# Splitting half of an output-projection weight during attention and keeping the parts in DRAM

## The chip, the cores and the metric

The kernel runs on one core of one Trainium2 chip. The metric is the device time of one execution in microseconds (us): before the change the median of three runs is 1147.73 us (1147.73 to 1148.61).

## The reference

One decoder block for 1024 tokens of 1024 features, in float32:

```python
h = rms_norm(x, g_attn_pre) * (1 + sc_a) + sh_a        # sc_a, sh_a, gt_a, ... from cond @ w_ada
proj = h @ w_in                                        # queries, keys, values of 16 heads
oa = banded_attention(qa, ka, va, 127, sink)           # mixer A: window, sink, 8 heads
ob = dilated_mixture_attention(qb, kb, vb)             # mixer B: 8 heads
mixed = concatenate([rms_norm(oa, g_mix_a), rms_norm(ob, g_mix_b)])
x = x + gt_a * rms_norm(mixed @ w_out, g_attn_post)
h = rms_norm(x, g_mlp_pre) * (1 + sc_m) + sh_m
x = x + gt_m * rms_norm(square(relu(h @ w_up)) @ w_down, g_mlp_post)
```

`w_out` is 1024 x 1024. The kernel folds the gains `g_mix_a`, `g_mix_b` into its rows.

## The kernel before

**Two parts for every number.** TensorE multiplies in a reduced format, so each operand is kept as a high part (the value rounded) and a low part (the rest), and every product takes three matmuls: high by high, low by high, high by low. Making the parts of a tile is called a split here: ScalarE (ACT) writes the high part, and VectorE (DVE), or GpSimd (POOL) where it is free, subtracts it from the value for the low part.

**Stages.** First the modulated, normalised `h` is made, transposed, and split into the tile `hw`, which has eight places of two parts of 128 x 1024. Then 18 projection tiles per half of the tokens (six units `u`, each of three 128-column tiles `c`, for two halves `x` of 512 tokens) are accumulated over eight chunks `k` of 128 features (`proj_mm`, lines 859 to 869, output tile `pj`). The attention of what is projected already runs beside it: scores (`s_ps`, L1127 for mixer B, L1182 for A), the running maximum on DVE (L1146, L1197), the exponential on ACT (L1153, L1202), the division on POOL (L1158, L1214), transposes on TensorE (PE; L1232 and L1235, L1239), the split of the transposed weights (`ph`: ACT L1246, DVE L1250), the product with the values (L1262 to L1267, L1274), and the sum of two halves into `ot` (ACT L1294 or L1309, DVE L1298 or L1314), stored to DRAM (`o_dram`, L1301, L1319). Projected tiles are rotated on DVE (L762 to L765), split (ACT L768, DVE or POOL L771), and sent through DMAs (L808) to the query and key tiles. POOL also works off 24 pieces of the modulation matrix beside attention (`ada_piece`: load L999, L1010 to L1015). After the last projection tile comes the output projection: per 128 tokens `o_sb` is loaded back from DRAM (L1423), split into `oh` and `ol` (ACT L1436, DVE L1439) and multiplied with the parts of `w_out` (`y_ps`, L1478 to L1480). Then follows the MLP, more than half of the time, which the change leaves as it is.

**What the split of `w_out` does before.** `hw` holds `h` until the projection is done, and the parts of `w_out` afterwards, chunk `k` in place `k`. In the old layout place `b` holds the 128 tokens of block `b` for all eight feature chunks, so a half of the tokens frees its four places together, at the last chunk of the last projection tile of that half (line 931, resource `r_wo`). `load_wo` (L1339) then takes, for each of the eight chunks: a load of 0.5 MB into a staging place (`wo_st`, L1348), the high part on ACT (L1353), and the low part on DVE (L1356) or on POOL in two instructions (L1361, L1362), whichever its planner finds earlier.

**The staging ring.** Five places of 128 x 1024 (`stage`, L444) serve, one after the other, the rotated tiles `hl`, the pieces `wa_st`, the rows of the rotation tables, `gate_st`, and `wo_st`. The planner counts free places (`r_stg`); which physical place a new tile gets is decided by the allocator of the pool, and the first instruction that writes the tile then waits for whoever used that place last.

**What sets the order.** One Python planner (`Sched`) writes each engine's instructions from modelled durations: it takes the step that can start first. The order is fixed when the program is built; on the chip each engine works its list in order, and an instruction that waits holds up all that stand behind it on its engine. All DMAs of this stage are issued by one queue, SyncE's (SP), in its order.

Of the kernel before, what the change touches and what calls it, by code (L numbers as in the profile page):

```python
# [10 lines left out]
F32 = mybir.dt.float32  # L11
F32R = mybir.dt.float32r
# [3 lines left out]
ALU = mybir.AluOpType  # L16
# [3 lines left out]
P = 128  # L20
D = 1024
S = 1024
KC = D // P
# [151 lines left out]
class Sched:  # L175
# [144 lines left out]
def t_sb(n):  # L320
    return 0.098 + 0.00083 * n
# [6 lines left out]
def t_dv(n):  # L328
    return 0.066 + 0.00104 * n
# [19 lines left out]
def hybrid_block(ctx: ExitStack, tc: tile.TileContext, x, positions, w_ada, b_ada, g_attn_post, w_in, w_out,  # L349
                 g_mlp_post, w_up, w_down, consts, out):  # L350
    nc = tc.nc
    ctx.enter_context(tc.manual_schedule())
    V, A, G, T = nc.vector, nc.scalar, nc.gpsimd, nc.tensor
    x, out = x[0], out[0]
    w_ada, w_out, w_up, w_down = w_ada[0], w_out[0], w_up[0], w_down[0]
    sc = Sched()
    op, pe_op = sc.op, sc.pe_op

    def pool(name, bufs=1, side="left", space=None, stack=ctx):
        kw = dict(name=name, bufs=bufs, reuse_waits="tile")  # L360
# [8 lines left out]
    dram = ctx.enter_context(tc.tile_pool(name="dram", bufs=1, space=DRAM))  # L369
# [5 lines left out]
    def ring_r(name):  # L375

        return ph2.right.tile([P, 1024], F32, name=name, tag="right")
# [7 lines left out]
    r_stg, r_w, r_wst, r_hl = Res(5), Res(WR), Res(WS), Res(0)  # L385
    r_u, r_raw, r_h2, r_wo = Res(0), Res(0), Res(0), Res(0)
# [8 lines left out]
    cols = head[:, CW_COL - 8:CW_COL + 56]  # L395
# [26 lines left out]
    hw = pool("hw", 1).tile([P, KC, 2, 1024], F32R, name="hw")  # L422
# [16 lines left out]
    st = Tok()  # L439
# [28 lines left out]
    xnT = p0.tile([P, KC, S], F32, name="xnT")  # L468
# [56 lines left out]
    w_raw, w_rawe, w_hl, w_e = {}, {}, {}, {}  # L525
# [45 lines left out]
    e = op("ACT", 0.1, lambda: A.activation(cond[:], c_raw, AF.Exp, scale=-1.0), [e_c], prio=0)  # L571
# [32 lines left out]
    e = op("DVE", 4.2, f_turns, [e_pos, e_c], prio=1)  # L604

    def f_sin():
# [5 lines left out]
                prio=1)  # L612
# [26 lines left out]
    def mod_group(g):  # L639
# [37 lines left out]
    def mod_chunk(k, eg, half):  # L677
        t0, t1 = (0, TB) if half is None else (4 * half, 4 * half + 4)
        n = (t1 - t0) * P
        ks = slice(k * P, (k + 1) * P)  # L680
# [11 lines left out]
        e = op("DVE", t_dv(n), lambda: V.tensor_tensor(hw[:, t0:t1, 1, ks], h, hh.bitcast(F32), ALU.subtract), [e],  # L692
               prio=0)
        for x in (0, 1) if half is None else (half,):
            e_hh[k, x], e_hl[k, x] = eh, e
# [6 lines left out]
    def tables(groups, place, r_place, r_bank, bank, deps):  # L702
# [30 lines left out]
       prio=8)  # L733

    qs, ks, vs, e_q, e_k, n_in = {}, {}, {}, {}, {}, {}
# [117 lines left out]
    def dense(dur, emit, deps, **kw):  # L853
        return pe_op("dense", dur, emit, deps, **kw)

    def w_at(u, c, k):
        return divmod(3 * k + c, 4) if u == 0 else (2 * c + k // 4, k % 4)

    def proj_mm(ps, u, c, k, x, part):
        i, n = w_at(u, c, k)  # L860
        t, w = slice(k * P, (k + 1) * P), w_hl[u, i]
        n = slice(n * P, n * P + P)
        h = [hw[:, 4 * x:4 * x + 4, i, t] for i in range(2)]
        ps = ps[:].rearrange("p (b t) -> p b t", t=P)
        if part != 1:
            T.matmul(ps, w[:, 0, n], h[0], start=(k == 0), stop=False)  # L866
            T.matmul(ps, w[:, 1, n], h[0], start=False, stop=False)  # L867
        if part != 0:
            T.matmul(ps, w[:, 0, n], h[1], start=False, stop=(k == KC - 1))  # L869
# [74 lines left out]
    todo_dense = [(u, x, c) for u in range(1, 6) for x in range(2) for c in range(3)]  # L944

    def feed_proj():
        if len(sc.pe.get("dense", [])) <= 4 and todo_dense:
            u, x, c = todo_dense.pop(0)
            if (x, c) == (1, 0):
                next_unit_w(u)  # L950
            if (u, x, c) == (2, 0, 0):
                for e_ in e_tab:
                    e_.clear()
                tables([(0, 1, 4)], lambda i: stage("rows")[:].rearrange("p (b r) -> p b r", b=TB), r_stg, r_x,
                       lambda: px.tile([P, 4, P], F32, name="ptab", tag="x"), [[e_rot[1, 0]], [e_rot[1, 1]]])
            proj_tile(u, x, c)
        return not todo_dense
# [29 lines left out]
    NADA = 24  # L987
    ada = Tok()
# [347 lines left out]
    NSTG2 = 4  # L1336
    ph2 = Tok()

    def load_wo():  # L1339

        if len(todo_dense) > 2 or ada.i < NADA:
            return False
        ph2.e_wo, ph2.raw = {}, {}
        eh = None
        for k in range(KC):
            def f_l(k=k):
                ph2.raw[k] = stage("wo_st")
                nc.sync.dma_start(ph2.raw[k][:], w_out[k * P:(k + 1) * P])  # L1348
            e = load(f_l, 524288, takes=[(r_stg, 1), (r_wo, 1)], prio=-8)
            g = cols[:, 56 + k:57 + k]  # L1350

            def f_h(k=k, g=g):
                A.mul(hw[:, k, 0], ph2.raw[k][:], g)  # L1353

            def f_lo(k=k, g=g):
                V.scalar_tensor_tensor(hw[:, k, 1], ph2.raw[k][:], g, hw[:, k, 0].bitcast(F32), ALU.mult,  # L1356
                                       ALU.subtract)
            eh = op("ACT", t_sb(D) + AP_COST, f_h, [e] + ([eh] if eh else []), prio=4)

            def f_lo2(k=k, g=g):  # L1360
                G.tensor_scalar(ph2.raw[k][:], ph2.raw[k][:], g, 1.0, ALU.mult, ALU.mult)  # L1361
                G.tensor_tensor(hw[:, k, 1], ph2.raw[k][:], hw[:, k, 0].bitcast(F32), ALU.subtract)  # L1362
            ph2.e_wo[k] = op(("DVE", "POOL"), (t_dv(D) + AP_DV, t_pts(D) + t_ptt(D)), (f_lo, f_lo2), [eh],
                             gives=[(r_stg, 1)], prio=4)
        return True

    def open_out():
# [13 lines left out]
        return True  # L1381

    sc.launch += [load_wo, open_out]
    h2, e_h2 = {}, {}

# [694 lines left out]
```

## Time and profile before

| | |
|---|---|
| median of three runs | 1147.73 us (1147.73 to 1148.61) |
| the profiled execution | 1148.87 us |
| its span, first to last instruction | 1147.1 us (1.8 us lie around it) |
| mean granted TensorE clock | 0.992 |
| DVE, ACT, POOL busy | 71%, 55%, 23% of the span |
| PE busy | 97% |
| last projection matmul / first `y_ps` | 377 us / 398.38 us after the start |

A profile page gives busy times by engine and groups of equal instructions. A row of the timeline has start and duration in us, the engine, the line of the kernel, output and inputs by the program's names, the number of instructions, and in brackets how long the engine was idle just before and what ended that. Matmuls overlap: one of 512 columns takes 0.39 us, and the next starts 0.23 us after it. A row of the windows view has a stretch of time, its length, then for PE, PEld, DVE, ACT and POOL the busy time in it and the number of instructions, then the granted TensorE clock (1.00 is full speed), the busy share of the DMA engines and GB/s.

### The profile page before, as it was taken

The numbers are of one execution on the slowest core, as the hardware profiler recorded it, in microseconds if no ns is written. First come the engines' busy times: TensorE is split into PE (matmuls) and PEld (weight loads), VectorE is DVE, ScalarE is ACT, GpSimd is POOL, SyncE is SP. The second block draws the span as 40 slices with busy tenths as digits, with TensorE's granted clock in tenths as the row PEclk, the third lists the DMA queues.
The fourth block names the chain that finished last, engine by engine and source line by source line (L and its number), as shares of the span: only waits on it lengthen the run. The fifth ranks groups of instructions, "written<-read, shape, count | busy, mean of one in ns | idle before, by whom it ended". The sixth has DMA issues, their size and how long they took to land.

```text
span 1147.1 us, 15609 instructions
## 1 busy us (share of the span) xinstructions
PE 1115.2 (97%) x5417; PEld 924.1 (81%) x5417; DVE 818.7 (71%) x1380; ACT 635.9 (55%) x1101; POOL 265.7 (23%) x349
## 2 busy tenths in 40 slices
PE   8999999999999899998999999999999999999996
PEld 7788878888888687887788888888888888888885
DVE  7878666666667765668979664599644896537998
ACT  8868865464556756675675424563234733246542
POOL 2458867565743521111000000000000000000002
PEclk9999999999999899998999999999999999999999
DMA  9556454343423305552981168812469112584103
GB/s 347 192 204 164 163 158 164 136 155 127 146 71 132 124 26 186 203 207 104 352 306 39 41 224 285 303 37 74 147 230 332 70 56 76 201 307 168 37 19 147
DMA packets 90910, 185.29 MB, mean 162 GB/s; under 512 B 8400, under 2 KB 31056, under 8 KB 90832
## 3 DMA queue, kind: packets, MB, share of 16 engines
q1 hardware_dynamic: 90832, 184.30, 46.3%
q8 instruction: 43, 0.70, 0.2%
q14 instruction: 35, 0.29, 0.1%
HBM read 137.08 MB, written 28.31 MB: 144 GB/s over the span
## 4 chain that ended last, share of the span: by engine, by line
PE 76%; DVE 8%; issue 4%; ACT 4%; POOL 4%; DMA 3%; SPq 1%; DVEq 0%; POOLq 0%; ACTq 0%
PE mlp_ps L1903 16%; PE mlp_ps L1904 16%; PE mlp_ps L1902 16%; PE pj L866 3%; PE pj L869 3%; PE pj L867 3%; PE s_ps L1127 3%; PE o_ps L1262 2%; PE pt_ps L1232 1%; PE y_ps L1478 1%; PE y_ps L1480 1%; PE y_ps L1479 1%; PE pt_ps L1235 1%; DVE hw L1673 1%; PE o_ps L1267 1%
## 5 line engine op out<-in xcount | busy, mean ns | idle before, releaser
L1902 PE MATMUL mlp_ps<-hw 128*128 128x512 f32 x896 | 350.7, 391 | 0.4 <-ACT hw L1664 0.4
L1903 PE MATMUL mlp_ps<-hw 128*128 128x512 f32 x896 | 349.5, 390 | 1.1 <-DVE hw L1670 1.1
L1904 PE MATMUL mlp_ps<-hw 128*128 128x512 f32 x896 | 349.4, 390 | 0.0
L1903 PEld LDWEIGHTS mlp_ps<-hw 128*128 128x128 f32 x896 | 168.7, 188 | 36.9 <-DVE hw L1670 1.4
L1902 PEld LDWEIGHTS mlp_ps<-hw 128*128 128x128 f32 x896 | 168.8, 188 | 36.4 <-ACT hw L1664 0.8
L1904 PEld LDWEIGHTS mlp_ps<-hw 128*128 128x128 f32 x896 | 168.6, 188 | 35.0
L1673 DVE TENSOR_TENSOR hw<-w,hw 128x1024 fp32r<-128x1024 f32 x96 | 114.7, 1221 | 95.1 <-ACT hw L1666 93.0
L1666 ACT CAST hw<-w 128x1024 fp32r<-128x1024 f32 x96 | 97.5, 1047 | 129.8 <-PE mlp_ps L1904 93.1
L2002 POOL TENSOR_TENSOR st<-st,nhalf 128x1 f32<-128x1 f32 x8 | 7.8, 977 | 604.1 <-DVE st L2000 604.1
L866 PE MATMUL pj<-hw,w_hl 128*128 128x512 f32 x240 | 102.5, 427 | 0.0
L869 PE MATMUL pj<-hw,w_hl 128*128 128x512 f32 x240 | 94.6, 394 | 0.0
L867 PE MATMUL pj<-hw,w_hl 128*128 128x512 f32 x240 | 94.5, 394 | 0.0
L1250 DVE TENSOR_TENSOR ph<-pt_ps,ph 128x512 fp32r<-128x512 f32 (+1 forms) x110 | 69.5, 648 | 34.6 <-ACT ph L1246 34.3
L1666 ACT CAST hw<-u 128x1024 fp32r<-128x1024 f32 x48 | 48.7, 1051 | 64.6 <-PE mlp_ps L1904 64.6
L1246 ACT CAST ph<-pt_ps 128x512 fp32r<-128x512 f32 (+1 forms) x110 | 58.9, 555 | 32.9 <-PE pt_ps L1235 27.5
L1153 ACT ACTIVATE p_sb<-p_sb,mn 128x128 f32<-128x128 f32 (+3 forms) x64 | 49.8, 778 | 38.3 <-DVE mn L1146 36.8
L1673 DVE TENSOR_TENSOR hw<-u,hw 128x1024 fp32r<-128x1024 f32 x48 | 57.1, 1220 | 18.2 <-ACT hw L1666 18.2
L1960 DVE TENSOR_TENSOR yacc<-yacc,mlp_ps 128x512 f32<-128x512 f32 x96 | 62.2, 683 | 3.3 <-PE mlp_ps L1904 3.3
L1158 POOL TENSOR_SCALAR p_sb<-p_sb,den 128x128 f32<-128x128 f32 (+3 forms) x64 | 48.4, 762 | 53.1 <-DVE den L1156 51.9
L1015 POOL TENSOR_TENSOR ada_acc<-ada_acc,wa_st 128x512 f32<-128x512 f32 x42 | 55.3, 1318 | 3.5
L869 PEld LDWEIGHTS pj<-hw,w_hl 128*128 128x128 f32 x240 | 45.1, 188 | 10.5
L1478 PE MATMUL y_ps<-hw,oh 128*128 128x512 f32 x128 | 51.7, 404 | 0.0
(206 smaller groups left out, 2010.4 us busy)
## 6 DMA issues: line engine op xcount, KB each, us to landing
hw<-s_dram SPq DMA_DIRECT2D x84, 512.0 KB, 4.4
wa_st<-in_w_ada SPq DMA_DIRECT2D x32, 512.0 KB, 4.4
w<-in_w_up SPq DMA_DIRECT2D x32, 512.0 KB, 4.8
w<-in_w_down SPq DMA_DIRECT2D x32, 512.0 KB, 7.5
s_dram<-hw SPq DMA_DIRECT2D x28, 512.0 KB, 4.3
qt<-hl SPq DMA_DIRECT2D x40, 256.0 KB, 2.8
w_st<-in_w_in SPq DMA_DIRECT2D x36, 256.0 KB, 3.1
x_sb<-in_x SPq DMA_DIRECT2D x16, 512.0 KB, 6.1
```

The lines of the kernel that those rows point to most:

```text
L866: T.matmul(ps, w[:, 0, n], h[0], start=(k == 0), stop=False)
L867: T.matmul(ps, w[:, 1, n], h[0], start=False, stop=False)
L869: T.matmul(ps, w[:, 0, n], h[1], start=False, stop=(k == KC - 1))
L1246: A.copy(b["ph"][:, 0, :w], b["pt"][:, :w])
L1250: V.tensor_tensor(b["ph"][:, 1, :w], b["pt"][:, :w], b["ph"][:, 0, :w].bitcast(F32), ALU.subtract)
L1478: T.matmul(ps[:], b["oh"][:, k], wh[:, c0:c0 + 512], start=(k == 4 * m), stop=False)
L1666: A.copy(out[j][0], flat(src[j]))
L1673: V.tensor_tensor(out[j][1], flat(src[j]), out[j][0].bitcast(F32), ALU.subtract)
L1902: T.matmul(ps[m][:], sh, mh, start=starts and k == 0, stop=False, **kw)
L1903: T.matmul(ps[m][:], sh, ml_, start=False, stop=False, **kw)
L1904: T.matmul(ps[m][:], sl, mh, start=False, stop=k == 3, **kw)
L1960: e = op("DVE", t_dv(512), lambda: V.tensor_tensor(y(), y(), ps[m][:], ALU.add), [e, ml.e_y[tb, n]], gives=gives, prio=1)
```

## The change

Three things are changed.

1. `h` lies in `hw` by feature chunks: place `4x + k//2`, and there columns 512 (`k%2`) to 512 (`k%2`) + 511, hold chunk `k` of the 512 tokens of half `x`. Every second `k` of the last projection tile of a half frees one place.
2. Chunks 4 to 7 of `w_out` are split during the attention stage, one after the other, as soon as the projection has passed 2.2, 3.0, 3.8 and 4.6 units (`st.d` counts them). `split_wo` takes two staging places for a chunk: the raw values (`wo_st`), into which DVE later writes the low part, and `wo_hi`, into which ACT writes the high part. Both are stored to DRAM (`wo_dram`, two DMAs of 0.5 MB).
3. `load_wo` splits chunks 0 to 3 as before, with the low part on DVE only. Chunks 4 to 7 are loaded from DRAM by two DMAs of 0.5 MB each, as their places in `hw` come free.

```diff
 def mod_chunk(k, eg, half):
-        h, hh = xnT[:, k, t0 * P:t1 * P].rearrange("p (b t) -> p b t", t=P), hw[:, t0:t1, 0, ks]
+        h = xnT[:, k, t0 * P:t1 * P].rearrange("p (x t) -> p x t", t=512)
+        hh, hl = (hw[:, t0 // 4 * 4 + k // 2:t1 - 3 + k // 2:4, i, k % 2 * 512:k % 2 * 512 + 512] for i in range(2))
...
 def proj_mm(ps, u, c, k, x, part):
-        h = [hw[:, 4 * x:4 * x + 4, i, t] for i in range(2)]
-        ps = ps[:].rearrange("p (b t) -> p b t", t=P)
+        h = [hw[:, 4 * x + k // 2, i, k % 2 * 512:k % 2 * 512 + 512] for i in range(2)]
...
-            if u == 5 and c == 2 and k == KC - 1:
-                gives.append((r_wo, 4))
+            if u == 5 and c == 2 and k % 2:
+                gives.append((r_wo, 1))
...
+    def split_wo(k):
+        raw, hi = [], []
+        g = cols[:, 56 + k:57 + k]
+        def f_l():
+            raw.append(stage("wo_st"))
+            nc.sync.dma_start(raw[0][:], w_out[k * P:(k + 1) * P])
+        e = load(f_l, 524288, takes=[(r_stg, 1)], prio=21)
+        def f_h():
+            hi.append(stage("wo_hi"))
+            A.mul(hi[0][:].bitcast(F32R), raw[0][:], g)
+        eh = op("ACT", t_sb(D) + AP_COST, f_h, [e], takes=[(r_stg, 1)], prio=9)
+        def f_lo():
+            V.scalar_tensor_tensor(raw[0][:].bitcast(F32R), raw[0][:], g, hi[0][:], ALU.mult, ALU.subtract)
+        el = op("DVE", t_dv(D) + AP_DV, f_lo, [eh], prio=9)
+        e_wod[k] = [load(lambda t=t, i=i: nc.sync.dma_start(wo_dram[k - 4][i][:], t[0][:]), 524288, [e_],
+                         gives=[(r_stg, 1)], prio=22) for i, (t, e_) in enumerate(((hi, eh), (raw, el)))]
+    def feed_wo():
+        k = 4 + len(e_wod)
+        if st.d > WO_AT[k - 4]:
+            split_wo(k)
+        return len(e_wod) == 4
+    WO_AT = (2.2, 3.0, 3.8, 4.6)
...
-        for k in range(KC):
+        for k in range(4):
...
-            ph2.e_wo[k] = op(("DVE", "POOL"), (t_dv(D) + AP_DV, t_pts(D) + t_ptt(D)), (f_lo, f_lo2), [eh],
-                             gives=[(r_stg, 1)], prio=4)
+            ph2.e_wo[k] = op("DVE", t_dv(D) + AP_DV, f_lo, [eh], gives=[(r_stg, 1)], prio=4)
+        for k in range(4, KC):
+            def f_d(k=k):
+                for i in range(2):
+                    nc.sync.dma_start(hw[:, k, i].bitcast(F32), wo_dram[k - 4][i][:])
+            ph2.e_wo[k] = load(f_d, 1048576, e_wod[k], takes=[(r_wo, 1)], prio=-8, n=2)
```

The planner writes other orders from this. Lines behind 1338 have other numbers in the changed kernel: the split ahead is L1348 (load), L1353 (ACT), L1357 (DVE) and L1359 (stores) there, the load from DRAM L1395, `o_sb` L1455 and `oh` L1468; lines between 927 and 1335 are one lower than before (L1246 is L1245).

The first place is ACT about 144 us after the start, at the end of the rotation tables (`tab`), where the first tile `hl` of unit 2 is split. Before:

```order
L723 ACTIVATE tab_147<-ptab,head 128x512
L768 COPY hl<-hl 128x512
L1309 COPY otmp<-o_ps 64x512
L1246 COPY ph<-pt_ps 128x512 x2
L1202 ACTIVATE p_sb,den_1870<-p_sb,mn_1869 128x257 x4
L779 ACTIVATE hl<-pj,head 128x512
```

And in the change:

```order
L723 ACTIVATE tab_147<-ptab,head 128x512
L1353 ACTIVATE wo_hi<-wo_st,head 128x1024
L768 COPY hl<-hl 128x512
L1308 COPY otmp<-o_ps 64x512
L1245 COPY ph<-pt_ps 128x512 x2
L1201 ACTIVATE p_sb,den_1880<-p_sb,mn_1879 128x257 x4
```

The first split ahead stands in front of the split of `hl`, the copy `otmp` and the two `ph`.

The second place is SP at the same time. Before, behind the load of a modulation piece came the key tile, `o_dram` and `gate_st`:

```order
L999 DMA wa_st<-in_w_ada 128x2x512
L808 DMA kt<-hl 32x2x512
L1319 DMA o_dram_110<-ot 64x2x128 x2
L1039 DMA gate_st<-in_b_ada 128x512
L1040 DMA gate_st<-in_g_attn_post 128x512
L808 DMA kt<-hl 32x2x512
```

In the change the load of `wo_st` and the store of its high part stand between:

```order
L998 DMA wa_st<-in_w_ada 128x2x512
L1348 DMA wo_st<-in_w_out 128x1024
L1359 DMA wo_dram_0_174<-wo_hi 128x1024
L808 DMA kt<-hl 32x2x512
L1318 DMA o_dram_110<-ot 64x2x128 x2
L1038 DMA gate_st<-in_b_ada 128x512
L1039 DMA gate_st<-in_g_attn_post 128x512
L1359 DMA wo_dram_1_175<-wo_st 128x1024
```

Here `wo_st` is also taken from the staging ring ahead of the tile `hl` that L762 writes, where before `hl` was the next to be taken.

The third place is ACT from the last value tile (`v_hl`, 384 us) to the first `oh`. Before, with four splits of `w_out`:

```order
L844 COPY v_hl<-pv 128x8x64
L1353 ACTIVATE hw<-wo_st,head 128x1024
L1246 COPY ph<-pt_ps 128x512
L1353 ACTIVATE hw<-wo_st,head 128x1024
L1294 COPY otmp<-o_ps 64x256
L1246 COPY ph<-pt_ps 128x384
L1353 ACTIVATE hw<-wo_st,head 128x1024 x2
L1294 COPY otmp<-o_ps 64x256
L1246 COPY ph<-pt_ps 128x512
```

And in the change:

```order
L844 COPY v_hl<-pv 128x8x64
L1245 COPY ph<-pt_ps 128x512
L1293 COPY otmp<-o_ps 64x256
L1245 COPY ph<-pt_ps 128x384
L1152 ACTIVATE p_sb,den<-p_sb,mn 128x640
L1245 COPY ph<-pt_ps 128x512
L1152 ACTIVATE p_sb,den<-p_sb,mn 128x768
```

The four splits are gone from it, and the rows of attention close up. On DVE two and on POOL two low parts are gone at the same place, and on PE the first `y_ps` stands 19 matmul rows later, behind more of the attention.

More of the change, by code (lines that the diff above doesn't have):

```diff
@@ L679, in mod_chunk @@
         n = (t1 - t0) * P
-        ks = slice(k * P, (k + 1) * P)
-        h, hh = xnT[:, k, t0 * P:t1 * P].rearrange("p (b t) -> p b t", t=P), hw[:, t0:t1, 0, ks]
+        h = xnT[:, k, t0 * P:t1 * P].rearrange("p (x t) -> p x t", t=512)
+        hh, hl = (hw[:, t0 // 4 * 4 + k // 2:t1 - 3 + k // 2:4, i, k % 2 * 512:k % 2 * 512 + 512] for i in range(2))
         deps = [eg] + (e_xn[0] + e_xn[1] if half is None else e_xn[half])
@@ L691, in mod_chunk @@
         e = op("ACT", t_sb(n) + 2 * AP_COST, full(A), [eh], prio=0)
-        e = op("DVE", t_dv(n), lambda: V.tensor_tensor(hw[:, t0:t1, 1, ks], h, hh.bitcast(F32), ALU.subtract), [e],
+        e = op("DVE", t_dv(n), lambda: V.tensor_tensor(hl, h, hh.bitcast(F32), ALU.subtract), [e],
                prio=0)
@@ L860, in proj_mm @@
         i, n = w_at(u, c, k)
-        t, w = slice(k * P, (k + 1) * P), w_hl[u, i]
-        n = slice(n * P, n * P + P)
-        h = [hw[:, 4 * x:4 * x + 4, i, t] for i in range(2)]
-        ps = ps[:].rearrange("p (b t) -> p b t", t=P)
+        w, n = w_hl[u, i], slice(n * P, n * P + P)
+        h = [hw[:, 4 * x + k // 2, i, k % 2 * 512:k % 2 * 512 + 512] for i in range(2)]
+        ps = ps[:]
         if part != 1:
@@ L1337, in hybrid_block @@
     ph2 = Tok()
+    wo_dram = [[dram.tile([P, 1024], F32, name=f"wo_dram{k}_{i}") for i in range(2)] for k in range(4, KC)]
+    e_wod = {}
+    def split_wo(k):
[20 more added lines that the diff above has]
+    WO_AT = (2.2, 3.0, 3.8, 4.6)
+    sc.launch.append(feed_wo)
     def load_wo():
-        if len(todo_dense) > 2 or ada.i < NADA:
+        if len(todo_dense) > 2 or ada.i < NADA or len(e_wod) < 4:
             return False
@@ L1358, in load_wo @@
             eh = op("ACT", t_sb(D) + AP_COST, f_h, [e] + ([eh] if eh else []), prio=4)
-            def f_lo2(k=k, g=g):
-                G.tensor_scalar(ph2.raw[k][:], ph2.raw[k][:], g, 1.0, ALU.mult, ALU.mult)
-                G.tensor_tensor(hw[:, k, 1], ph2.raw[k][:], hw[:, k, 0].bitcast(F32), ALU.subtract)
-            ph2.e_wo[k] = op(("DVE", "POOL"), (t_dv(D) + AP_DV, t_pts(D) + t_ptt(D)), (f_lo, f_lo2), [eh],
-                             gives=[(r_stg, 1)], prio=4)
+            ph2.e_wo[k] = op("DVE", t_dv(D) + AP_DV, f_lo, [eh], gives=[(r_stg, 1)], prio=4)
[4 more added lines that the diff above has]
+            ph2.e_wo[k] = load(f_d, 1048576, e_wod[k], takes=[(r_wo, 1)], prio=-8, n=2)
         return True
```

## The prediction

> **What bounds the kernel now.** I first read the busy times of the page.
>
> ```profile
> PE 1115.2 (97%) x5417; PEld 924.1 (81%) x5417; DVE 818.7 (71%) x1380; ACT 635.9 (55%) x1101; POOL 265.7 (23%) x349
> ```
>
> TensorE is the bound nearly everywhere, so the change can only give or take time where PE waits or where its clock falls. Second comes the windows view around the places where PE waits longest, with the granted clock before the DMA share and GB/s.
>
> ```profile
> 391.00:394.40 3.40, 1.77 (x8) 1.37 (x9) 3.40 (x10) 2.23 (x6) 3.32 (x2) 0.99 0.42 144
> 394.40:401.20 6.80, 6.24 (x22) 4.98 (x21) 4.83 (x14) 5.30 (x9) 4.20 (x5) 0.50 0.34 103
> 527.50:530.90 3.40, 1.07 (x5) 0.56 (x3) 2.50 (x3) 0.47 (x1) 2.90 (x1) 1.00 0.15 59
> 530.90:537.70 6.80, 6.07 (x19) 5.10 (x20) 3.66 (x10) 5.31 (x7) 0.00 (x0) 0.50 0.00 0
> 544.50:548.00 3.50, 2.02 (x8) 1.15 (x7) 3.50 (x6) 3.50 (x8) 0.00 (x0) 1.00 0.31 128
> ```
>
> After 3.4 us in which PE was busy for 52% (1.77 of 3.40) or 31%, the clock was 0.50 for 6.8 us; after 58% (2.02 of 3.50) it stayed at 1.00. A wait of over about 1.5 us in one such stretch therefore costs twice: itself, and half of 6.8 us of work. The first of the two places is the one the change works on. Third, the timeline of PE there, rows with a wait:
>
> ```profile
> 387.63 0.39 PE L1262 MATMUL o_ps<-ph,v_hl 128*128 128x256 f32 x1 [0.80 <-DVE ph L1250]
> ...
> 391.07 0.38 PE L1262 MATMUL o_ps<-ph,v_hl 128*128 128x256 f32 x1 [0.56 <-ACT ph L1246]
> 392.78 0.39 PE L1262 MATMUL o_ps<-ph,v_hl 128*128 128x256 f32 x1 [1.33 <-DVE ph L1250]
> ...
> 393.85 0.80 PE L1127 MATMUL s_ps<-kt,qt 128*128 128x512 f32 x2 [0.23 <-DVE mn L1146]
> ...
> 396.09 0.48 PE L1232 MATMUL pt_ps<-head,p_sb 128*128 128x128 f32 x1 [0.16 <-POOL p_sb L1158]
> 396.97 0.48 PE L1232 MATMUL pt_ps<-head,p_sb 128*128 128x128 f32 x1 [0.40 <-POOL p_sb L1158]
> ...
> 398.38 0.78 PE L1478 MATMUL y_ps<-hw,oh 128*128 128x512 f32 x1
> ```
>
> Six waits, 3.48 us in all. The rows of the engines they name show what stood in front:
>
> ```profile
> 387.82 2.19 ACT L1353 ACTIVATE hw<-wo_st,head 128x1024 fp32r<-128x1024 f32 x2
> ...
> 390.43 0.59 ACT L1246 CAST ph<-pt_ps 128x512 fp32r<-128x512 f32 x1
> ...
> 389.31 2.49 DVE L1356 SCALAR_TENSOR_TENSOR hw<-wo_st,head,hw 128x1024 fp32r<-128x1024 f32 x1
> ...
> 395.22 2.47 POOL L1158 TENSOR_SCALAR p_sb<-p_sb,den 128x640 f32<-128x640 f32 x3
> ...
> 382.09 6.28 SPq L1301 DMA_DIRECT2D o_dram<-ot  x3
> 391.82 0.33 SPq L1377 DMA_DIRECT2D gate_a<-gate_d  x1
> 392.26 0.38 SPq L1423 DMA_DIRECT2D o_sb<-o_dram  x1
> ```
>
> `ph` (390.43) waits behind two splits on ACT, its low part behind one on DVE until 391.72, three divisions on POOL wait for its splits until 395.22, and `o_sb` stands on SP behind `gate_a`, whose place the same DVE split frees.
>
> **Term 1, the transition: -5.8 us.** The change takes four ACT splits, two DVE low parts and two POOL pairs out of this stretch, by the groups
>
> ```profile
> L1353 ACT ACTIVATE hw<-wo_st,head 128x1024 fp32r<-128x1024 f32 x8 | 8.9, 1146 | 0.0
> L1356 DVE SCALAR_TENSOR_TENSOR hw<-wo_st,head,hw 128x1024 fp32r<-128x1024 f32 x5 | 8.0, 1626 | 0.0
> ```
>
> 4 x 1.15 us of ACT and 1.28 + 2.49 = 3.77 us of DVE. At most this gives the 3.48 us of waits and, if no 3.4 us stretch is then emptier than 58%, the half clock: 6.24 us busy at 0.50 are 3.1 us of full work. Sum 6.6. Late next is attention's own chain from scores to `ph`, which has no projection matmuls to hide behind any more; I leave it the three waits that name the maximum and the division, 0.23 + 0.16 + 0.40 = 0.79, so the term is -5.8. The first `y_ps` moves behind more attention but isn't short of data: `o_sb` no longer waits for 391.72; the `o_dram` stores ahead of it are issued by 388.37, and `o_sb` needs 4.4 us itself (its row stands in the next part), so `oh` can come 2 us or so earlier than in the trace. If the half clock stays, only some 2.2 is left (3.48 less waits of 1.3).
>
> The loads from DRAM are not late: the places come free while the last tile is projected, which ends about 377, and the eight loads of 0.5 MB have until about 396. Their cover is over 10 us.
>
> **Term 2, the first split ahead: +4.6 us.** Around it the trace has these rows of five engines, and behind them, from the view of DMA issues, one 0.5 MB load by itself near 139 us and the two of the transition, time to landing last.
>
> ```profile
> 144.30 1.29 POOL L1015 TENSOR_TENSOR ada_acc<-ada_acc,wa_st 128x512 f32<-128x512 f32 x1
> ...
> 145.63 0.68 DVE L762 TENSOR_TENSOR hl<-pj,tab 64x512 f32<-64x512 f32 x1 [4.88 <-POOL ada_acc L1015]
> ...
> 150.42 1.29 DVE L1250 TENSOR_TENSOR ph<-pt_ps,ph 128x512 fp32r<-128x512 f32 x2
> ...
> 156.43 0.69 DVE L1045 TENSOR_TENSOR gate_st<-ada_ps,gate_st 128x512 f32<-128x512 f32 x1 [1.01 <-DMA gate_st<-in_b_ada]
> ...
> 143.54 0.67 ACT L723 ACTIVATE tab<-ptab,head 128x512 f32<-128x512 f32 x1
> 148.55 0.62 ACT L768 CAST hl<-hl 128x512 fp32r<-128x512 f32 x1 [4.34 <-POOL wa_st L1014]
> ...
> 149.40 0.74 PE L1182 MATMUL s_ps<-kt,qt 128*128 128x256 f32 x4 [1.78 <-DVE mn L1197]
> ...
> 151.37 0.64 PE L1274 MATMUL o_ps<-ph,v_hl 128*128 128x512 f32 x2
> ```
> ```profile
> wa_st<-in_w_ada SPq DMA_DIRECT2D x1, 512.0 KB, 3.7
> ...
> gate_a<-gate_d SPq DMA_DIRECT2D x1, 512.0 KB, 3.2
> o_sb<-o_dram SPq DMA_DIRECT2D x1, 512.0 KB, 4.4
> ```
>
> In the trace the tile `hl` waits 4.88 us for a staging place that POOL reads until 145.59. In the change `wo_st` is taken from the ring just before `hl`, so I take it that `wo_st` gets this place and `hl` the next, which is free. Then DVE rotates `hl` at once and PE's 1.78 us go. But the load of `wo_st` starts at 145.6, lands at 149.3, and the split keeps ACT until 150.5. Behind it on ACT stand `hl` (148.55 before), `otmp` and two `ph`: all 1.95 us later. The first low part of `ph`, done at 151.05 before, comes at 153.0, and so does the PE row L1274 (151.37 before): 1.65 us lost. PE reaches this row 1.78 us earlier, at 149.6, so it stands for 3.45 us in one piece. However that falls over two stretches of 3.4 us, one has at least 1.7 us of it and is busy for at most 50%; the trace's clock fell after 52%. A period of 6.8 us at 0.50, up to 1.7 us of it still within the wait, costs (6.8 - 1.0) / 2 = 2.9. Together 4.6.
>
> Ends of this term: -1.8, if `wo_st` gets a place that is free; +5.1, if the whole half-clock period is work; and 3.1 without the half clock, since the next is then late: SP issues `gate_st` behind the store of the high part, so L1045 comes 2.8 us late and the `ph` behind it on DVE 3.1 us.
>
> The Trainium skill, "TensorE: Matmul & The Clock Gate", section "What's actually happening", says that the clock falls to half after at least one idle window of about 3.4 us, free-running. The 6.8 us above are two such windows, which agrees; but here a window busy for 52% was enough. Taken at its word, an idle window, the rule would spare the half clock after 3.45 us of waiting, and the term would be 3.1; that is rival A.
>
> **Term 3, the other three splits: +0.5 us.** ACT has room for them:
>
> ```profile
> 199.23 0.37 ACT L1294 COPY otmp<-o_ps 64x256 f32<-64x256 f32 x1 [3.68 <-PE o_ps L1265]
> ...
> 248.40 0.59 ACT L1246 CAST ph<-pt_ps 128x512 fp32r<-128x512 f32 x1 [1.47 <-PE pt_ps L1235]
> ...
> 293.14 1.16 DVE L1250 TENSOR_TENSOR ph<-pt_ps,ph 128x512 fp32r<-128x512 f32 x2 [1.02 <-ACT ph L1246]
> ...
> 294.16 0.40 PE L1262 MATMUL o_ps<-ph,v_hl 128*128 128x256 f32 x2
> ```
>
> By the program's order the second split stands ahead of the row at 199.23, the third ahead of 248.40, the fourth shortly ahead of the `ph` whose low part runs at 293.14; 1.15 us fit into 3.68 and into 1.47. On DVE each low part takes 1.28 to 2.49. With it the `ph` of the third and fourth come about 0.7 us later, against a slack of 0.44 (the first of the two rows at 293.14 ends at 293.72, PE uses it at 294.16): some 0.25 each, so 0.5 in all, 0 to 2.0 if each takes 2.49. If the cover of ACT goes (a load landing 1 us late), 1 us more.
>
> The Trainium skill, "SBUF — State Buffer", section "SBUF: two separate sides", says that a DVE instruction with two SBUF inputs and a GpSimd one that reads SBUF exclude each other for a whole instruction. The row of 2.49 us beside POOL's splits agrees with that, and it speaks against the new low parts, which run beside POOL's modulation pieces: by it they take the upper end, 2.0 us.
>
> **Terms at nothing.** The new layout of `h` makes the moving operand contiguous.
>
> ```profile
> L1903 PE MATMUL mlp_ps<-hw 128*128 128x512 f32 x896 | 349.5, 390 | 1.1 <-DVE hw L1670 1.1
> ...
> L869 PE MATMUL pj<-hw,w_hl 128*128 128x512 f32 x240 | 94.6, 394 | 0.0
> L1478 PE MATMUL y_ps<-hw,oh 128*128 128x512 f32 x128 | 51.7, 404 | 0.0
> ```
>
> `y_ps` reads its moving operand contiguously already and takes 404 ns, `pj` with four blocks 394, so there is nothing to gain: 0. The lower end is the 4 ns by which `pj` is above the MLP's 390, on 6 x 2 x 3 x 8 x 3 = 864 matmuls: 3 us. One low part of chunks 0 to 3 goes from POOL to DVE near 350 us, where PE waits for nothing over 0.2 us: 0. The new loads and stores beside the projection cost what terms 2 and 3 say, and nothing else.
>
> **Sum.** -5.8 + 4.6 + 0.5 = -0.7 us. The profiled execution took 1148.87 (span 1147.1 and 1.8 around it), 1.14 above the median of 1147.73; its change applied to the median gives **1147.0**. That is no change: about 0.2%, 2.3 us, is what a measurement of this kernel can tell.
>
> **Rivals.**
> - A, faster. The half clock isn't granted after the first split's wait: term 2 is 3.1, the sum -2.2, 1145.5. For it: the gap may fall across two windows evenly. Against: 52% was enough at 391. Chance 0.18. Or `wo_st` finds a free place and nothing waits: term 2 is between -1.8 and 0, the sum about -6, 1141.9. Against it: the wait of 4.88 us shows which place comes next. Chance 0.10.
> - B, slower. The transition keeps a wait of 1.5 us or more in one 3.4 us stretch, from which point the clock falls to half there too. With nothing but attention left, the chain through DVE, ACT, POOL and back takes longer than PE's work; before the first of those splits the trace has such waits as well. Then term 1 is -2.2, and -2.2 + 4.6 + 0.5 = +2.9: 1150.6. Against it: what is removed stood in front of just the rows that PE waited for. Chance 0.22.
> - C, the change doesn't do what it says: the stores hold up SP until its queue, not ACT, sets the transition, and the chunks from DRAM come after `oh`; each 1 us that `y_ps` waits beyond 396 is 1 us, from 1.5 us on with the half clock. Some +3, 1150.6. Against it is a cover of over 10 us. Chance 0.08.
>
> **Chances and range.** The forecast has 0.42; of it 0.05 ends faster and 0.05 slower by over 0.2%. A adds 0.20 to faster and 0.08 to the same, B 0.18 to slower and 0.04 to the same, C 0.07 to slower, 0.01 to the same: faster 0.25, same 0.45, slower 0.30. The likeliest case alone reaches from 1145.7 (term 1 at 6.6, term 3 at 0) to 1149.0 (term 2 at 5.1, term 3 at 2.0). The range for 8 in 10 goes from A's second case, 1142.0, to B with term 3 at its upper end, 1152.0.
>
> **What would show it.** Right: in the changed profile PE waits 3 to 4 us near 150 for `ph`, with ACT's split behind the landing of `wo_st`, and the granted clock is 0.50 in the next 6.8 us; near 386 to 396 the waits shrink to 1 us and the clock stays at 1.00; the first `y_ps` stands near 401 with the earlier loss of 4.6 in it. Wrong: `wo_st` loaded before 145; the clock at 0.50 near 396; a wait of `y_ps` for `hw`; or waits of over 1 us at the other three splits.

## The result and the profile after

| | before | after |
|---|---|---|
| median of the runs of the first comparison | 1147.98 us (1146.44 to 1151.07, 16 runs) | 1145.09 us (1144.15 to 1147.21, 16 runs) |
| ratio, with its 95% interval | | 0.9978 (0.9971 to 0.9985) |
| the profiled execution | 1148.87 us | 1147.21 us |
| its span; mean granted clock | 1147.1 us; 0.992 | 1145.4 us; 0.993 |

The change makes the kernel faster by 0.22% by the ratio, 2.9 us between the medians, where 0.7 us was forecast and called no change. A second comparison gave 0.9982 (0.9972 to 0.9993), 1.8 us between the medians. The profiled execution after is the slowest of its 16, so the two profiles differ by 1.7 us only.

First the busy line of the page of the changed kernel: TensorE is again busy 97% of the span and 1.1 us less than before. Then its windows view (PE, PEld, DVE, ACT and POOL busy, granted clock, DMA share, GB/s), at the first split ahead, at the transition and near 531 us.

```profile
PE 1114.1 (97%) x5417; PEld 922.6 (81%) x5417; DVE 821.1 (72%) x1382; ACT 635.5 (55%) x1099; POOL 258.2 (23%) x346
```
```profile
148.70:152.10 3.40, 1.29 (x6) 0.72 (x4) 0.21 (x1) 2.46 (x4) 3.32 (x7) 1.00 0.22 88
152.10:158.90 6.80, 6.38 (x14) 4.29 (x15) 4.44 (x9) 4.44 (x13) 2.71 (x5) 0.50 0.70 204
...
391.00:394.40 3.40, 3.40 (x24) 2.70 (x23) 3.37 (x14) 2.69 (x7) 1.08 (x2) 1.00 0.10 24
394.40:401.20 6.80, 5.99 (x39) 4.92 (x39) 5.76 (x14) 5.59 (x11) 2.35 (x3) 1.00 0.33 98
527.50:530.90 3.40, 0.65 (x3) 0.19 (x1) 2.04 (x3) 0.92 (x1) 2.44 (x1) 1.00 0.01 1
530.90:534.40 3.50, 3.22 (x12) 2.93 (x13) 2.07 (x7) 3.50 (x6) 0.00 (x0) 0.51 0.00 0
```

The half clock has moved: 6.8 us of it now follow the first split ahead, none is left at the transition, and near 531 us it is 3.4 us in place of 6.8. The rows of the first split, from the timeline of four engines of the changed kernel:

```profile
144.83 1.30 POOL L1014 TENSOR_TENSOR ada_acc<-ada_acc,wa_st 128x512 f32<-128x512 f32 x1
146.16 0.35 SPq L1348 DMA_DIRECT2D wo_st<-in_w_out  x1
...
149.59 1.15 ACT L1353 ACTIVATE wo_hi<-wo_st,head 128x1024 fp32r<-128x1024 f32 x1 [4.88 <-DMA wo_st<-in_w_out]
150.64 0.60 ACT L768 CAST hl<-hl 128x512 fp32r<-128x512 f32 x1
151.27 0.58 ACT L1308 COPY otmp<-o_ps 64x512 f32<-64x512 f32 x1
151.88 1.07 ACT L1245 CAST ph<-pt_ps 128x512 fp32r<-128x512 f32 x2
...
142.21 0.69 DVE L762 TENSOR_TENSOR hl<-pj,tab 64x512 f32<-64x512 f32 x1 [0.95 <-ACT tab L723]
152.50 1.29 DVE L1249 TENSOR_TENSOR ph<-pt_ps,ph 128x512 fp32r<-128x512 f32 x2
154.10 1.28 DVE L1357 SCALAR_TENSOR_TENSOR wo_st<-wo_st,head,wo_hi 128x1024 fp32r<-128x1024 f32 x1
```
```profile
147.88 0.72 PE L1181 MATMUL s_ps<-kt,qt 128*128 128x256 f32 x4
...
152.52 0.79 PE L1273 MATMUL o_ps<-ph,v_hl 128*128 128x512 f32 x1 [2.53 <-ACT ph L1245]
```

The load starts when POOL's last read of the place ends (144.83 + 1.30 = 146.13), the split waits for it until 149.59, and `hl`, `otmp` and `ph` follow it on ACT. DVE rotates `hl` at 142.21 without its former wait of 4.88 us, and PE reaches the scores of L1181 without the former 1.78. Then it stands 2.53 us for the high part of `ph`. At the transition PE's rows with a wait of over 0.3 us, and the first `y_ps`, are:

```profile
385.93 0.66 PE L836 MATMUL pv<-head,vt 128*128 128x128 f32 x4 [0.41 <-DVE ot L1297]
387.51 0.33 PE L1231 MATMUL pt_ps<-head,p_sb 128*128 128x128 f32 x1 [0.81 <-POOL p_sb L1157]
389.04 0.51 PE L1261 MATMUL o_ps<-ph,v_hl 128*128 128x256 f32 x2 [0.35 <-DVE v_hl L847]
397.15 0.39 PE L1261 MATMUL o_ps<-ph,v_hl 128*128 128x256 f32 x1 [0.39 <-DVE ph L1249]
399.03 0.39 PE L1261 MATMUL o_ps<-ph,v_hl 128*128 128x256 f32 x1 [0.34 <-DVE ph L1249]
...
406.31 0.39 PE L1261 MATMUL o_ps<-ph,v_hl 128*128 128x256 f32 x1 [0.32 <-DVE ph L1249]
```
```profile
400.20 0.47 PE L1510 MATMUL y_ps<-hw,oh 128*128 128x512 f32 x1
```

The first three stand in before too; of the six waits that the prediction counted nothing over 0.4 us is left.

The matmuls are the same in both kernels, so the start of each, after less before, says where time went. Medians over stretches (us), for the first profile of the change and its second (the experiment "the change again"):

| stretch | forecast | first | second |
|---|---|---|---|
| up to 140 us | 0 | +0.5 | +0.3 |
| first split ahead, 140 to 160 | +4.6 | +3.2 | +3.2 |
| a wait for a store of `ot` near 193, gone | 0 | -0.8 | -0.8 |
| other three splits, 200 to 340 | +0.5 | +1.5 | +1.0 |
| transition, 340 to 500 | -5.8 | -4.9 | -4.6 |
| half clock near 531 | 0 | -1.3 | -1.2 |
| sum | -0.7 | -1.8 | -2.1 |

### The profile page after: what moved, and what is told of

It reads as the page before. It is cut to its first block, busy times and chain, and to the rows that moved or that the text cites. A ratio compares the mean times of both kernels' runs of the same rounds, so it can differ in the third digit from the quotient of the medians.

```text
span 1145.4 us, 15658 instructions
## 1 busy us (share of the span) xinstructions
PE 1114.1 (97%) x5417; PEld 922.6 (81%) x5417; DVE 821.1 (72%) x1382; ACT 635.5 (55%) x1099; POOL 258.2 (23%) x346
## 4 chain that ended last, share of the span: by engine, by line
PE 74%; DVE 9%; ACT 5%; DMA 4%; issue 4%; POOL 3%; SPq 0%; DVEq 0%; POOLq 0%; ACTq 0%
PE mlp_ps L1935 16%; PE mlp_ps L1936 16%; PE mlp_ps L1934 16%; PE pj L865 4%; PE pj L866 4%; PE pj L868 4%; PE s_ps L1126 3%; PE o_ps L1261 1%; PE pt_ps L1231 1%; DVE hw L1705 1%; PE pt_ps L1234 1%; DMA wo_st<-in_w_out 1%; PE o_ps L1266 1%; DVE x_sb L2036 1%; PE o_ps L1273 1%
## 5 line engine op out<-in xcount | busy, mean ns | idle before, releaser
L1245 ACT CAST ph<-pt_ps 128x512 fp32r<-128x512 f32 (+1 forms) x110 | 58.9, 555 | 26.7 <-PE pt_ps L1234 20.5
```

The costliest lines, as they stand in the source:

```text
L1245: A.copy(b["ph"][:, 0, :w], b["pt"][:, :w])
```

## The experiments

Ratios are to the kernel before, run on the same chip. Line numbers are those of each kernel.

**1. The first split ahead later.** It comes at 2.35 units in place of 2.2; `e11` is the same kernel again.

```diff
-    WO_AT = (2.2, 3.0, 3.8, 4.6)
+    WO_AT = (2.35, 3.0, 3.8, 4.6)
```

> The changed kernel with the first of the four splits ahead only after 2.35 instead of 2.2 projected units (the other three as they are). It then stands some 20 us later on ScalarE, behind the rotated tile hl, which gets the staging place that POOL still reads, as in the kernel before. Theory (the changed kernel's gain at the transition, about 4.9 us in its profile, is partly spent at the first split, where PE waits 2.5 us for ph behind the load of wo_st and then runs at half clock for 6.8 us, 3.2 us in all): this costs nothing here, PE waits 1.8 us near 148 as before, the clock stays at 1.00 there, and the time is some 3 us below the changed kernel, 1142 us, 0.995 of before. Rival (the half clock is a matter of where the windows fall and not of this wait; the split's place is indifferent): no difference to the changed kernel, 0.9978, within 0.0007.

> The first split ahead at 2.35 in place of 2.2 once more, beside the run in which only its ScalarE and VectorE splits move. Theory: 0.9945 to 0.9965 again, with the 1.74 us wait of the kernel before near 148 and no half clock there. Rival (its first ratio of 0.9955 was luck with the half clock): 0.9975 or more.

Measured: 0.9955 (0.9938 to 0.9972), 1143.89 us; again: 0.9966 (0.9952 to 0.9979), 1144.14 us. PE is back at the wait of the kernel before, with no half clock behind it, first from the timeline and then from the windows of the first of the two:

```profile
149.73 0.74 PE L1181 MATMUL s_ps<-kt,qt 128*128 128x256 f32 x4 [1.74 <-DVE mn L1196]
```
```profile
147.00:150.40 3.40, 1.66 (x14) 1.42 (x13) 3.27 (x11) 1.47 (x3) 3.32 (x4) 1.00 0.01 2
150.40:153.80 3.40, 3.40 (x15) 2.42 (x14) 2.82 (x7) 3.37 (x11) 1.72 (x5) 1.00 0.33 90
```

Against the runs of before beside them, these two lie 4.2 and 4.0 us lower by the medians, the change 2.9 and 1.8: the place of the first split costs some 1 to 2.5 us. That is less than the 3 us expected; the second ratio is just above the range named for it, and its interval overlaps that of the change. The place at 2.35 isn't free either: in the second of the two profiles ACT's split begins at 170.56, 8.8 us after the issue of its load, DVE's low part follows at 171.82, and PE waits 1.99 us at 172.3 for the maximum behind it.

**2. Layout and early release alone.** Of the change, only the new layout of `h` and its release by twos; all eight chunks are loaded and split at the transition as before.

```diff
-            if u == 5 and c == 2 and k == KC - 1:
-                gives.append((r_wo, 4))
+            if u == 5 and c == 2 and k % 2:
+                gives.append((r_wo, 1))
```

> Only the new layout of h and the release of one place at every second chunk; all eight chunks of w_out are loaded and split as before, with no split ahead and nothing kept in DRAM. Theory 1 (the gain comes from taking four of the splits out of the end of the projection): the splits still have to run between 372 and 390 us, PE waits for ph as before and the clock falls; 0.999 to 1.001. Theory 2 (the gain comes from places that come free earlier, so that the same splits run beside the last projection tile): PE's waits near 386 to 397 go, the clock stays at 1.00 there, and since no split stands near 150 either the time is 3 to 5 us below before, 0.996 to 0.997, below the changed kernel.

Measured: 1.0016 (1.0005 to 1.0027), 1150.64 us. That the early release alone brings the gain falls: the last four splits come some 4 us earlier on average, and now stand ahead of `ot`, for which the value matmuls wait, with 6.8 us of half clock behind it. DVE and PE:

```profile
384.81 2.21 DVE L1355 SCALAR_TENSOR_TENSOR hw<-wo_st,head,hw 128x1024 fp32r<-128x1024 f32 x1 [0.36 <-ACT hw L1352]
386.94 0.41 DVE L1297 TENSOR_TENSOR ot<-o_ps,otmp 64x256 f32<-64x256 f32 x1
```
```profile
387.41 0.66 PE L836 MATMUL pv<-head,vt 128*128 128x128 f32 x4 [2.46 <-DVE ot L1297]
```

**3. The splits ahead without their use.** The change with its splits and stores, but chunks 4 to 7 loaded from `w_out` and split at the transition all the same, with GpSimd's low parts as before.

```diff
-        for k in range(4):
+        for k in range(KC):
...
-        for k in range(4, KC):
-            def f_d(k=k):
-                for i in range(2):
-                    nc.sync.dma_start(hw[:, k, i].bitcast(F32), wo_dram[k - 4][i][:])
-            ph2.e_wo[k] = load(f_d, 1048576, e_wod[k], takes=[(r_wo, 1)], prio=-8, n=2)
```

> The changed kernel with its four splits ahead and their stores, but all eight chunks of w_out are loaded and split at the transition as in the kernel before (the parts in DRAM are not used). It prices the splits ahead: by the first theory 3.2 us at the first split and about 0 to 1 at the other three on top of the layout-and-release kernel that runs beside it. Rival (splits ahead are hidden behind PE): the same time as that kernel, within 0.5 us.

Measured: 1.0047 (1.0031 to 1.0064), 1154.09 us: 3.5 us above experiment 2, which differs from it by the splits ahead. That is their price by the medians of 7 and 11 runs; where it lies this profile doesn't show, since it is the fastest of its 7 (1149.67 to 1156.91). It has both bad places, 2.43 us at 150 for `ph` and, as in experiment 2, 2.45 us at the transition:

```profile
386.35 0.93 PE L836 MATMUL pv<-head,vt 128*128 128x128 f32 x4 [2.45 <-DVE ot L1297]
```

**4. One split ahead.** Only chunk 4 is split ahead, at 4.6 units, and its parts are loaded for chunks 4 to 7, so three chunks' splits are left out.

```diff
-    WO_AT = (2.2, 3.0, 3.8, 4.6)
+    WO_AT = (4.6,)
...
-                    nc.sync.dma_start(hw[:, k, i].bitcast(F32), wo_dram[k - 4][i][:])
+                    nc.sync.dma_start(hw[:, k, i].bitcast(F32), wo_dram[0][i][:])
```

> The changed kernel with only one split ahead, of chunk 4, at 4.6 units; its two parts are loaded for all of the chunks 4 to 7 (three chunks' splits are left out, so the output is not the reference's). The loads from DRAM and the rest are the same. It prices the transition by itself: if the transition gives 4.9 us and the first split costs 3.2, this kernel is 4.5 to 5 us below before, 0.996, and 2 to 3 below the changed kernel, with PE's wait near 148 still 1.8 us as before. Rival (the splits ahead cost nothing): the same as the changed kernel, 0.9978.

Measured: 0.9957 (0.9942 to 0.9972), 1143.79 us, with no wait of `y_ps` for `hw`. It doesn't differ measurably from experiment 1, which has three splits more, so these three, at 2.35, 3.0 and 3.8 units, cost little. By the starts of the same matmuls between 220 and 340 us experiment 1 loses nothing at its last two splits, the change 1.2 and 0.7.

**5. The first split without its wait for the load.** ACT's place for it is the same; only its input is another, resident tile.

```diff
-            A.mul(hi[0][:].bitcast(F32R), raw[0][:], g)
+            A.mul(hi[0][:].bitcast(F32R), hw[:, 4, 0].bitcast(F32) if k == 4 else raw[0][:], g)
```

> The changed kernel; the first split ahead (chunk 4) keeps its place on ScalarE and its load, but its ScalarE instruction reads a resident tile of h in place of the loaded wo_st, so it waits for no load (the high part of chunk 4 is that of other data). Theory (the load that waits for its staging place is what costs there): the wait of 2.53 us near 150 us goes to under 0.8 us, the clock stays at 1.00, the ratio to before is about 0.995 and the stretch up to 180 us is 3 us shorter than in the changed kernel. Rival (the 1.15 us of ScalarE and 1.28 us of VectorE work in that place cost, whenever the load lands): a wait of 1.5 us or more stays near 150, and the ratio is 0.9975 or more.

Measured: 0.9952 (0.9938 to 0.9967), 1143.94 us. PE doesn't wait at all between 145 and 155 us (ACT's row, and a window):

```profile
144.06 1.14 ACT L1353 ACTIVATE wo_hi<-hw,head 128x1024 fp32r<-128x1024 f32 x1
```
```profile
148.40:151.80 3.40, 3.40 (x15) 2.43 (x14) 3.01 (x7) 2.72 (x10) 3.40 (x4) 1.00 0.89 334
```

One operand of one instruction is all that differs, and between 140 and 180 us the kernel is 4.3 us shorter than the change (-1.15 against +3.19). ACT's 1.14 us in that place cost PE nothing; waiting there for the load does. Behind it only a wait of 0.77 us comes at 157 us, for a `ph` that stands on DVE behind a wait for the load of `gate_st`.

**6. Load at its place, split later.** The load takes its place in the ring at 2.2 units as in the change, the two splits of the chunk come at 2.3, behind `hl`, `otmp` and both `ph`.

```diff
-        if st.d > WO_AT[k - 4]:
+        if k not in raws and st.d > WO_LD[k - 4]:
+            load_wos(k)
+        if k in raws and st.d > WO_AT[k - 4]:
             split_wo(k)
...
-    WO_AT = (2.2, 3.0, 3.8, 4.6)
+    WO_LD = (2.2, 3.0, 3.8, 4.6)
+    WO_AT = (2.3, 3.0, 3.8, 4.6)
```

> The changed kernel with the first chunk's load at its place (2.2) and its ScalarE and VectorE splits later (2.3, behind hl, otmp and both ph). Theory (only the wait for the load in front of ph costs; the staging place that the load takes spares hl its wait of 4.9 us): no wait over 1 us near 148 to 152, clock 1.00 there, the stretch up to 180 us about 1.5 us shorter than in the kernel before, ratio to before 0.993 to 0.995, below that of the split moved as a whole. Rival (moving only the split leaves hl or ph waiting for the place that the raw tile keeps longer): a wait of 1.5 us or more before 160, ratio 0.9955 or more.

Measured: 0.9941 (0.9928 to 0.9953), 1141.43 us: 6.7 us under the kernel before, the fastest of all, and its interval lies below that of the change. DVE's and ACT's rows, and a window:

```profile
141.79 0.69 DVE L762 TENSOR_TENSOR hl<-pj,tab 64x512 f32<-64x512 f32 x1 [0.95 <-ACT tab L723]
```
```profile
147.53 1.08 ACT L1245 CAST ph<-pt_ps 128x512 fp32r<-128x512 f32 x2
...
149.98 1.14 ACT L1358 ACTIVATE wo_hi<-wo_st,head 128x1024 fp32r<-128x1024 f32 x1
```
```profile
148.40:151.80 3.40, 3.40 (x15) 2.44 (x14) 2.66 (x6) 3.40 (x11) 3.32 (x5) 1.00 0.51 149
```

The load lands behind other work of ACT, and `hl` has the next, free place: the wait of the kernel before goes and none takes its place.

**7. The release of four at once.** The early release is taken out of the change.

```diff
-            if u == 5 and c == 2 and k % 2:
-                gives.append((r_wo, 1))
+            if u == 5 and c == 2 and k == KC - 1:
+                gives.append((r_wo, 4))
```

> The changed kernel with the places of h released four at once, as before, in place of two k at a time. Theory (what gains at the transition is that chunks 4 to 7 need no ScalarE and VectorE split there; the early release only spares loads that are hidden): the four stores come back in 5 us or so and y_ps isn't late, the ratio to before stays within 0.996 to 0.9985. Rival (the release by twos carries the gain): the four splits of chunks 0 to 3 and the loads move to 378 us and later, waits of 3 us return between 380 and 400, ratio 1.000 or more.

Measured: 0.9978 (0.9969 to 0.9988), as the change, though in its profile PE has one wait of 1.63 us for `ot` at 392 us with 3.4 us of half clock behind it. The early release gives no gain that can be measured, with the splits ahead or, by experiment 2, without them.

**8. The change again**, for a second profile.

> The changed kernel once more, for a second profile and its runs on this chip. Theory (PE's wait at the first split is the same in every run, and only the length of the half clock after it differs, 3.4 or 6.8 us): a wait of 2.3 to 2.7 us near 150 for ph, the clock 0.50 behind it for 3.4 or 6.8 us, ratio 0.997 to 0.9985. Rival (the 2.53 us of the first profile are one run's accident): a wait under 1.5 us and no half clock near 152, ratio about 0.995.

Measured: 0.9982 (0.9972 to 0.9993). Again 2.53 us of wait and 6.8 us of half clock behind them. In experiments 3 and 7 the same wait, 2.43 and 2.49 us, was followed by 3.4 us only.

**9. The kernel before without GpSimd's low parts**, twice.

```diff
-            ph2.e_wo[k] = op(("DVE", "POOL"), (t_dv(D) + AP_DV, t_pts(D) + t_ptt(D)), (f_lo, f_lo2), [eh],
-                             gives=[(r_stg, 1)], prio=4)
+            ph2.e_wo[k] = op("DVE", t_dv(D) + AP_DV, f_lo, [eh], gives=[(r_stg, 1)], prio=4)
```

> The kernel before, with the eight low parts of w_out on VectorE alone (GpSimd's pairs of two chunks dropped). Theory (the splits stand in front of ph on ScalarE and VectorE): the four ScalarE splits stay ahead of the ph rows and VectorE has more in front of them, so the waits of 387 to 397 us stay 3 us or more, the clock still falls to 0.50, and the ratio to before is 0.999 to 1.003. Rival (GpSimd's splits, which delay its divisions and slow VectorE's low part to 2.49 us, are the cause): the waits shrink to about 1 us, no half clock, ratio about 0.995.

> The kernel before with the low parts on VectorE alone, once more. Theory (what the edit itself gives is the 1.5 us of its first profile at the transition; the 0.8 us near 193 and the 1.2 us near 531 are chance): ratio 0.998 to 0.9995, and at the transition again VectorE's low part at 1.28 us in place of 2.49, the wait of 1.33 us near 392 down to 0.3, and the half clock still there. Rival (the edit gives all of what was measured): ratio 0.9965 to 0.998 again, with no wait near 193 and 3.4 us of half clock near 531.

Measured: 0.9976 (0.9964 to 0.9987), then 0.9971 (0.9960 to 0.9981): both theories missed it in the first run, and mine in the second too. One edit of the change, at its transition, gives as much as the whole change. DVE's low part runs without POOL beside it, and the `ph` behind it comes sooner (DVE and PE of the first run):

```profile
388.72 1.28 DVE L1356 SCALAR_TENSOR_TENSOR hw<-wo_st,head,hw 128x1024 fp32r<-128x1024 f32 x1
```
```profile
391.21 0.38 PE L1262 MATMUL o_ps<-ph,v_hl 128*128 128x256 f32 x1 [0.34 <-DVE ph L1250]
```

1.28 us in place of 2.49, and 0.34 us of wait in place of 1.33. Between 340 and 500 us this gives 1.8 us in the first profile, where the half clock stayed, and 3.1 in the second, where it didn't come. The rest lies where the edit changes no instruction: 0.8 us near 193, where DVE's `ot` waits for the landing of a store in both profiles of before (PE then 0.70 and 2.05 us) and in neither of these, and 1.2 to 1.3 near 531. Whether the first of these is chance isn't settled: of the fourteen profiles the wait near 193 stands in four, the two of before and experiments 2 and 4 (PE 1.57 and 1.58 us).

**10. The kernel before again**, for a second profile.

> The kernel before once more, for a second profile. Theory (the clock gate near 531 us works in free-running stretches of 3.41 us, so whether the wait for the last x rows costs one or two of them is chance): the wait of 3.0 us near 528 is there, the half clock behind it lasts 3.4 or 6.8 us; near 391 the wait of 1.3 us and the half clock come back. Rival (the 6.8 us belong to the kernel before): 6.8 us again, as in its first profile.

Measured: 1149.79 us. Near 391 the wait (1.32 us) and 6.8 us of half clock came back. Near 528 the wait is 3.05 us again, but the clock stays up behind it; 3.4 us of half clock come at 548, behind a wait of 1.15 us. So the 6.8 us near 531 don't belong to the kernel before.

## Why the prediction was right and wrong

The forecast, -0.7 us, lies 2.2 us above the measured difference of the medians; the measured time is within the range. The mechanisms were those of the text; the sizes of all three terms were off. That they add up to -0.2 and -0.4 in the two profiles, near the -0.7, is partly luck: the errors of +0.9, -1.4 and +1.0 (+1.2, -1.4 and +0.5) cancel.

**Term 1, -5.8, came as -4.9 and -4.6.** The waits behind the splits went as counted and the clock stayed at 1.00, so rival B didn't come, nor rival C: the first `y_ps`, at 400.20, waits for nothing. What is left isn't the 0.79 us kept for the maximum and the division but three waits for DVE's part of `ph` (397.15, 399.03 and 406.31), 1.05 us. That the splits had to leave ACT is not the whole cause: experiment 9 gets 1.8 to 3.1 us by freeing POOL alone. The prediction named POOL's share in the 2.49 us row but sized no rival by it. How the gain divides between the two is open, since no run moves the four splits and leaves GpSimd's low parts in place.

**Term 2, +4.6, came as +3.2.** The place of the ring, the landing (3.4 us behind the issue, 3.7 said), the order on ACT, the half clock of 6.8 us and the wait that it replaces are as forecast; experiments 5 and 6 show that the wait for the load is the cause. The step that failed is "The first low part of `ph`, done at 151.05 before, comes at 153.0, and so does the PE row": PE's row waited for ACT's high part alone and started at 152.52, when DVE's low part had only begun (152.50). The wait was 2.53 us, not 3.45, the loss against before 0.75, not 1.65. The half clock then has the other 2.4, where 2.9 were said.

**Term 3, +0.5, came as +1.5 and +1.0**: 0.3 at a new wait of 0.4 us for ACT's `ph` near 216 us, far from any split, 0.8 and 0.5 at the third split, and 0.4 and 0.2 at the fourth, where 0.25 each were said. What failed is ACT's cover at the third split, and the prediction had named that condition, a load landing late: the load came 5.8 us behind its issue, ACT waited 1.08 us for it (0.75 in the second profile), DVE for ACT, and PE for the `ph` behind.

```profile
251.25 1.15 ACT L1353 ACTIVATE wo_hi<-wo_st,head 128x1024 fp32r<-128x1024 f32 x1 [1.08 <-DMA wo_st<-in_w_out]
...
252.44 1.28 DVE L1357 SCALAR_TENSOR_TENSOR wo_st<-wo_st,head,wo_hi 128x1024 fp32r<-128x1024 f32 x1 [1.87 <-ACT wo_hi L1353]
...
254.38 0.39 PE L1261 MATMUL o_ps<-ph,v_hl 128*128 128x256 f32 x1 [0.58 <-DVE ph L1249]
```

It is the cost of the first split again, on a smaller scale. In both profiles of experiment 1 ACT doesn't wait at the third split, and nothing is lost there. The upper end of 2.0 wasn't reached: none of the low parts took 2.49 us. Two of the four ran with no POOL instruction beside them (1.28 us); the two that overlapped one took 1.28 and 1.55, and 1.57 and 1.45 in the second profile.

**Not in the sum:** the 0.8 us near 193, where the change moves no split (though SP's list is another, with the load of the second split at 193.80), and the 1.3 us near 531, where it touches nothing. They are 2.1 us together, as much as the measured gain of these profiles. The prediction took the stretches away from the change as fixed. Two profiles of one program show that they aren't: the two profiles of before differ by 1.3 us near 193.

**Rival A's first case** (no half clock behind the first split's wait) didn't come in any of the four profiles with that wait, though twice it lasted half as long. Its second case, a free place, is what experiments 5 and 6 make by hand: by the medians -4.4 and -6.7 us.

## What to carry to other kernels

Work that is moved ahead into a gap of an engine cost little by its own time here, but the instruction that consumes a load holds everything behind it until the load lands: issue the load at the early place and put the consumer behind the engine's urgent work. Leave room for the landing: loads of the same 0.5 MB came 3.4 us (first split), 5.8 us (third split) and 8.7 us (experiment 1 again) behind their issue. Ask also which engine slows which: taking a helper engine's share away gave as much here as moving half the work. And below 0.3% compare many runs, and more than one profile, since waits and clock at untouched places move by a microsecond.

## What the runs showed of the hardware

In these traces the granted clock falls at the ends of stretches of 3.413 us that run on by themselves: in the profile of before it fell at 394.37 and 530.90, 40 stretches apart, in that of the change at 152.08 and 530.96, 111 apart. Where the clock didn't fall in between, they are counted from the trace's ends (experiment 1 again: it rose at 6.86 and fell at 1136.67, 331 apart). What a wait costs depends on where it falls among them. The busy share of PE is worked out from its rows in the stretch that ends where the clock fell, or, where it didn't fall, in the emptiest:

| place and kernel | wait, us | busy share | half clock behind it, us |
|---|---|---|---|
| 148, experiment 1; 4 | 1.74; 1.78 | 0.49; 0.48 | none |
| 150, the change twice | 2.53 | 0.39; 0.37 | 6.83 |
| 150, experiments 3; 7 | 2.43; 2.49 | 0.33; 0.27 | 3.41 |
| 391, before twice | 1.3 and smaller ones | 0.51; 0.45 | 6.83 |
| 391, experiment 9 twice | 0.3 to 0.8 each | 0.67; 0.66 | 6.83; none |
| 528, before; again | 3.06; 3.05 | 0.32; 0.43 | 6.83; none |
| 528, the change; experiment 1 again | 3.03; 3.05 | 0.18; 0.54 | 3.41; none |

The prediction's "the trace's clock fell after 52%" is no threshold: at 0.43 to 0.54 it stayed up in four cases of the table, and at 0.67 it fell once. A wait of 3.05 us that spread over two stretches (0.54 and 0.56) cost no clock at all. The windows of the second profile of before show such a spread near 528. The windows begin some 0.25 us before the two stretches, whose shares are 0.67 and 0.43:

```profile
527.50:530.90 3.40, 2.54 (x12) 1.77 (x10) 3.40 (x5) 1.04 (x2) 2.50 (x1) 1.00 0.58 236
530.90:534.30 3.40, 1.21 (x10) 1.17 (x11) 1.07 (x3) 2.41 (x4) 0.96 (x1) 1.00 0.00 0
```

At these two places, 150 and 528 us, the half clock lasted 6.83 us where the wait reached 0.39 us or more into the next stretch, and 3.41 us where it reached 0.22 us or less. What besides the busy share decides whether the clock falls is open; no run here tells it apart.
